# Neighbourhood attention in pairs of heads: the exponential's bias from the pass with the maximum, one split and one transposition for two heads

## The chip, the cores and the metric

The kernel runs on one core of one Trainium2 chip. The metric is the device time of one execution in microseconds (us); lower is better. TensorE (PE) multiplies matrices, VectorE (DVE), ScalarE (ACT) and GpSimd (POOL) work on elements, and SyncE (SP) issues DMAs. PE reads from SBUF and writes to PSUM.

## The reference

One encoder layer over 1024 tokens of width 1024, a grid of 16 rows and 64 columns. The normalised input is projected to two head groups: group A is grouped-query attention, group B is neighbourhood attention with 8 heads of 64. Each group is gated, the two are concatenated and projected, the residual is added and a final norm follows. Group B, cut to what matters:

```python
k_rows = lax.dynamic_slice_in_dim(kg, r0, kh, axis=1)      # 8 rows of keys for a query row
sc = jnp.einsum('bjqhd,bkjchd->bhjqkc', qb, k_band) * scale
sc = jnp.where(mask, sc + bias, -jnp.inf)                  # learned bias by 2-D offset, 16 columns
p = jax.nn.softmax(sc, axis=(-2, -1))
o = jnp.einsum('bhjqkc,bkjchd->bjqhd', p, v_band)
o_b = o_b * jax.nn.silu(g_b)
mixed = jnp.concatenate([o_a, o_b], axis=-1)
x = x + mixed @ w_out
```

## The kernel before

Numbers are kept as pairs of 16-bit floats, a high part and a low part, and a product takes three matmuls: high by high, high by low, low by high. Tokens are cut into 8 units of 128 queries (`u`). In group B a unit sees its own 128 keys and those of the two units beside it: 384 keys, or 256 for the first and the last unit. The order is `ORDER`, units 0, 7, 1, 2, 3, 4, 5, 6, and the 8 heads of a unit one after the other. The first sixteen heads are so the narrow ones.

The stage of group B is 64 steps, one for a head, with a tail of 6. A step is written by `Flow.step` and `run_units`:

- `b_qk` makes the scores of two heads at once on PE (in every other step; `sb` tiles, four PSUM banks). For its own head DVE adds the bias of the offsets, keeps the sum `t` and takes its maximum (L825), and multiplies the maximum by minus the scale and adds a constant (L827, 128x1). ACT takes the exponential twice from `t`: as 32-bit `p32` (L828) and as 16-bit high part (L829).
- `b_lo` of the head before subtracts the two on DVE for the low part (L834). SP then issues one DMA that transposes both parts (L838, 6 blocks of 128x128) into a `ptb` place.
- Jobs that are due on DVE, then filling matmuls on PE (L482, in chunks of six; `FILL_B_END` chunks a step, the rest carried over): gate projections (`pj` tiles) and then output projections (`po` tiles), which share two PSUM buffers.
- `b_pv`, five heads later (six from step `MORE` on), multiplies the transposed parts with the values on PE (L851 to L853). After the fourth head of a group DVE divides by the sum and POOL multiplies with the gate.

Within a stage each engine does its instructions in the order in which the steps write them. Work that is not attention stands in lists of jobs: `job(engine, cost, ..., delay)` puts it into the step that lies `delay` steps ahead, jobs of ACT at the start of that step and jobs of DVE after `b_lo`; `BASE_B` says how much of a step is left for those that may wait. Three kinds of job matter here:

- A filling tile that is done is emptied one step later: for a gate ACT takes tanh (L682) and DVE multiplies (L687); for an output DVE adds to the residual (L961). The tile after the next one takes its buffer.
- `os_start` prepares a finished unit for the output projection. Squares (ACT L888, DVE L892) and a power on POOL, then ACT writes the two halves of the high part (L900), one step apart, and DVE the low halves behind them (L904). Then two DMAs transpose the parts of `mhl` (L913), and the output tiles of that unit can begin. `SPLIT_AT` says in which step it starts.
- Weights of a later group are squared (ACT L350), and split into high (ACT L392) and low parts (DVE L397), a quarter at a time.

Of the kernel before, what the change touches and what calls it, by code (L numbers as in the profile page):

```python
# [16 lines left out]
P = 128  # L17
KC = 8
NU = 8
# [15 lines left out]
PREP = {2: 4, 3: 0, 4: 2}  # L35
NEG = -1.0e38
EPS = 1e-6
# [101 lines left out]
def kernel(ctx: ExitStack, tc: tile.TileContext, x: bass.AP, w: bass.AP, wo: bass.AP,  # L139
# [203 lines left out]
    def squares(g, delay):  # L343

        wss[g] = [tn(f"wss{g}_{k}", 1, "ws") for k in range(4)]

        def quarter(i):
            o = (carve(ar, 16384 + SLOTS["th"][0] + (0 if "six" in late else (turn.get("th", 0) + 1) % 2) * SLOTS["th"][1], [512], BF16)
                 if "b" in late else va_more)
# [329 lines left out]
    def g_gen(g, up, mix, cols, isb):  # L679
        def evac(pt):  # L680
            th = slot("th" if "b" in late else "tha", [P, 2, GC], F32)
            job("act", 0.7, lambda: act.activation(th, pt, AF.Tanh, scale=col(G2 + g - GATE)), late=0)  # L682
# [129 lines left out]

    def b_qk(i, u, h):
        hh, h4i = divmod(h, 4)
# [6 lines left out]
        hl = t.bitcast(F16).rearrange("p (a b) -> p a b", a=2)  # L821
        assert ("bias", int(0 < u < NU - 1), hh, h4i) in ready
        b = bias[hh][:, h4i, (a - u + 1) * P:(a - u + 1 + n) * P]
        mx = tn(f"mx{u}_{h}")
        dve.tensor_tensor_reduce(out=t, in0=s, in1=b, scale=1.0, scalar=-3e38,  # L825
                                 op0=OP.add, op1=OP.max, accum_out=mx)
        dve.tensor_scalar(mx, mx, col(NSB + hh), LN_P, op0=OP.mult, op1=OP.add)  # L827
        act.activation(p32, t, AF.Exp, bias=mx, scale=col(SCB + hh))  # L828
        act.activation(hl[:, 0], t, AF.Exp, bias=mx, scale=col(SCB + hh))  # L829
        hls["b", u, h] = (hl, p32)  # L830

    def b_lo(i, u, h):
        hl, t = hls.pop(("b", u, h))
        dve.tensor_tensor(hl[:, 1], t, hl[:, 0], op=OP.subtract)  # L834
        k = i - MORE + 5
        pt = (area(32896, [2 * keys(u)[1], P], F16) if k >= 0 and k % 6 == 5 else
              slot("ptb", [P, 2 * keys(u)[1], P], F16))
        sp.dma_start_transpose(pt, hl.rearrange("p a b -> p (a b)"))  # L838
        pts["b", u, h] = pt

    def b_pv(i, u, h):
        hh = h // 4
# [5 lines left out]
        o = pv["b", u, hh][:, h % 4]  # L848
        pt = pts.pop(("b", u, h))
        for c in range(n):  # L850
            pe.matmul(o, pt[:, c], vb[hh][:, a + c, h % 4, v_hi], start=c == 0, stop=False)  # L851
            pe.matmul(o[:, :D], pt[:, c], vb[hh][:, a + c, h % 4, v_lo], start=False, stop=False)
            pe.matmul(o, pt[:, n + c], vb[hh][:, a + c, h % 4, v_hi], start=False, stop=c == n - 1)  # L853
        if h % 4 == 3:
            def evac():
# [5 lines left out]
                dve.tensor_tensor(s4, s4, col(VF + 4 * hh, 4), op=OP.mult)  # L861
                ot = slot("ob", [P, 4, D], F32)
                dve.tensor_tensor(ot, pv["b", u, hh][:, :, :D], s4[:, :, None].to_broadcast([P, 4, D]), op=OP.mult)
# [224 lines left out]

    def run_units(units, skew, qk, lo, pvf, n, hooks=None, by_hand=0, more=1000):

        m, hand = len(units), ExitStack()
        for i in range(m + skew + (more < 1000)):
            back = skew + (i >= more)
            if i == by_hand:
                hand.enter_context(tc.manual_schedule(engines={e.engine for e in (act, dve, pool, sp)}))
            first = (lambda: qk(i, *units[i])) if i < m else None
            second = (lambda: lo(i - 1, *units[i - 1])) if 1 <= i <= m else None
            last = (lambda: pvf(i - back, *units[i - back])) if i >= back and i != more else None
            if qk is a_qk:
                first, last = (lambda f=first, l=last: [g() for g in (f, l) if g]), None  # L1100
            if hooks:
                hooks(i)
            fl.step(n(i), first, second, last)
            sums_now()
        return hand
# [9 lines left out]
    fl.base = BASE_A  # L1115
    with run_units(ua, SKEW_A, a_qk, a_lo, a_pv, rates(FILL_A + [(64 - n_head, mid)], FILL_A_END), by_hand=HAND):
        pass
# [11 lines left out]

    ub = [(u, h) for u in ORDER for h in range(NH)]  # L1130

    late["b"] = True
    def hooks(i):
        if i == 0:
            late["r"] = [one.tile([P, 3072], F16, tag=f"r{j}", name=f"rest{j}") for j in range(2)]
            outer, late["inner"] = [t[:, 2048:2816].bitcast(F32) for t in late["r"]]
            make = load_bias(1, outer)
            sp.dma_start(late["inner"], headmask)
            for h in range(4):
                job("dve", 0.5, make, h, delay=h, late=0)  # L1140
        if i == 1:
            prep(13)
        if NH < i <= 2 * NH:
            at(1, "post", narrow, i - NH - 1)
        if i == 46:
            late["gout"] = one.tile([P, 1024], F32, tag="gain", name="gain_o")
            sp.dma_start(late["gout"], dap(gain_out, 0, [[0, P], [1, 1024]]))
# [17 lines left out]
    def hooks2(i):  # L1165
        hooks(i)
        if i == MORE - 2:
            late["six"] = True
        for u, k in zip(ORDER, SPLIT_AT):
# [5 lines left out]
    fl.base = BASE_B  # L1175
    with run_units(ub, SKEW_B, b_qk, b_lo, b_pv, rates(FILL_B, FILL_B_END), hooks2, more=MORE):
        pass
# [92 lines left out]
```

## Time and profile before

| | us |
|---|---|
| median of 3 runs (572.87 to 575.61) | 575.24 |
| span of the profiled execution, first to last instruction | 570.8 |
| own time of the profiled execution | not printed; 2 to 5 above its span if it was like the three runs |
| stage of group B, first maximum to last product with the values | 370.8 to 536.4 |
| PE busy over the span | 517.2 (91%) |
| DVE busy | 459.4 (80%) |
| ACT busy | 391.7 (69%) |
| mean granted clock of PE | 0.979 |

Busy times are sums of records. A PE that is recorded as busy is not always at its peak, and an instruction of DVE may start some hundredths of a microsecond before the one ahead of it ends. A wait is put down to the engine that ended last before it. The chain that ended last is mostly a list of small pieces here, so the stage is best read from waits, from the source views and from the timeline.

### The profile page before, as it was taken

What the parts mean: (1) busy time and instruction counts of PE and PEld (TensorE: products, weight loads), DVE (VectorE), ACT (ScalarE), POOL (GpSimd) and SP (SyncE); (2) the same over time, 40 slices, a digit from 0 to 9 for tenths busy, and PEclk for the clock granted to TensorE, in tenths of its full rate; (3) what the DMA queues carried; (4) which work ended last, traced back from release to release, by engine and by line L of the source; (5) the groups of instructions that cost most, each with busy time, mean ns of one, the idle gap of its engine ahead of it and who ended that gap; (6) DMA issues with size and microseconds to landing.
All of it is one profiled execution on the core that took longest, in us unless ns stands there. A gap on an engine that the chain in (4) does not pass through costs nothing. (4 is left out here: it accounts for less than half of the span.)

```text
span 570.8 us, 13962 instructions
## 1 busy us (share of the span) xinstructions
PE 517.2 (91%) x5583; PEld 402.1 (70%) x5583; DVE 459.4 (80%) x1018; ACT 391.7 (69%) x615; POOL 150.6 (26%) x181
## 2 busy tenths in 40 slices
PE   2678889969999999999999999999799799997994
PEld 0456777757887555568888888887677577776883
DVE  4688787989887988778779887589978998988852
ACT  5546457667777769687696886387888888875321
POOL 2395786650000000000000022334521311212210
PEclk9979999998999999999999999999989899999998
DMA  8999548779999989998998999436466999899842
GB/s 241 220 175 231 121 91 185 131 144 165 220 180 210 158 204 200 197 196 162 217 191 192 184 160 213 132 52 130 121 121 107 198 216 165 144 176 167 194 109 73
DMA packets 245539, 95.49 MB, mean 167 GB/s; under 512 B 236513, under 2 KB 237025, under 8 KB 243554
## 3 DMA queue, kind: packets, MB, share of 16 engines
q1 hardware_dynamic: 241874, 73.89, 71.1%
q0 software_dynamic: 3312, 19.92, 12.7%
q10 hardware_dynamic: 288, 0.79, 0.5%
q8 instruction: 43, 0.70, 0.5%
q14 instruction: 22, 0.18, 0.1%
HBM read 29.56 MB, written 4.19 MB: 59 GB/s over the span
## 5 line engine op out<-in xcount | busy, mean ns | idle before, releaser
L482 PE MATMUL pj<-whl,hT 128*128 128x256 f16 x2112 | 254.9, 278 | 26.1 <-DMA hT<-ar 9.2
L482 PEld LDWEIGHTS <-hT 128*128 128x128 f16 x2112 | 203.7, 99 | 63.6 <-issue 20.3
L722 ACT ACTIVATE ar<-s,nm,sm 128x1024 f32<-128x1024 f32 x64 | 76.9, 1201 | 56.5 <-DVE nm L720 56.2
L720 DVE CUSTOM_DVE_ANT_0 ar<-s,sm 128x1024 bf16<-128x1024 f32 x64 | 82.0, 1281 | 35.0 <-PE s L715 34.6
L482 PEld LDWEIGHTS <-ar 128*128 128x128 f16 x768 | 73.0, 99 | 16.1 <-issue 7.0
L728 DVE TENSOR_TENSOR ar<-ar 128x1024 f16<-128x1024 f32 x64 | 80.3, 1255 | 0.9 <-ACT ar L723 0.8
L482 PE MATMUL po<-whl,ar 128*128 128x256 f16 x576 | 68.7, 273 | 2.0 <-DVE x2b L961 1.8
L723 ACT ACTIVATE ar<-ar 128x1024 f16<-128x1024 f32 x64 | 67.6, 1057 | 1.9
L828 ACT ACTIVATE rq<-ar,mx,sm 128x384 f32<-128x384 f32 (+1 forms) x64 | 43.0, 672 | 25.3 <-DVE mx L827 25.0
L829 ACT ACTIVATE ar<-ar,mx,sm 128x384 f16<-128x384 f32 (+1 forms) x64 | 43.5, 680 | 2.1
L482 PE MATMUL kb<-hT,whl 128*128 128x512 f16 x192 | 44.5, 379 | 0.0
L834 DVE TENSOR_TENSOR ar<-rq,ar 128x384 f16<-128x384 f32 (+1 forms) x64 | 35.5, 555 | 8.2 <-ACT ar L829 8.0
L746 PE MATMUL pv<-va,ar 128*128 128x64 f16 x384 | 40.6, 195 | 0.0
L745 PE MATMUL pv<-va,ar 128*128 128x65 f16 x384 | 40.5, 194 | 0.0
L747 PE MATMUL pv<-va,ar 128*128 128x65 f16 x384 | 40.4, 193 | 0.0
L713 PE MATMUL s<-kTa,rq 128*128 128x512 f16 x128 | 38.5, 383 | 1.5 <-ACT ar L722 1.4
L745 PEld LDWEIGHTS <-ar 128*128 128x128 f16 x384 | 35.9, 97 | 5.5 <-issue 0.3
L397 DVE SCALAR_TENSOR_TENSOR whl<-raw,sm,whl 128x512 f16<-128x512 f32 x52 | 39.5, 790 | 0.0
L746 PEld LDWEIGHTS <-ar 128*128 128x128 f16 x384 | 35.7, 98 | 5.5 <-issue 0.3
L207 POOL DMA_DIRECT2D raw<-in_w_dram x11 | 6.7, 607 | 113.0 <-ACT ar L723 88.8
L747 PEld LDWEIGHTS <-ar 128*128 128x128 f16 x384 | 35.7, 99 | 0.0
L392 ACT ACTIVATE whl<-raw,sm 128x512 f16<-128x512 f32 x52 | 33.9, 708 | 0.0
(163 smaller groups left out, 918.8 us busy)
## 6 DMA issues: line engine op xcount, KB each, us to landing
raw<-in_w_dram POOLq DMA_DIRECT2D x11, 1024.0 KB, 7.4
raw<-in_wo_dram POOLq DMA_DIRECT2D x4, 1024.0 KB, 5.7
ar<-in_x_dram SPq DMA_DIRECT2D x7, 512.0 KB, 6.3
khh<-ar SPq DMA_DIRECT2D x16, 128.0 KB, 3.5
x2b<-in_x_dram POOLq DMA_DIRECT2D x4, 512.0 KB, 6.1
x<-in_x_dram POOLq DMA_DIRECT2D x4, 512.0 KB, 5.8
out_dram<-x2b SPq DMA_DIRECT2D x8, 256.0 KB, 4.8
ar<-ar SPq DMA_TRANSPOSE x112, 4.3
```

The source lines that it names most:

```text
L397: dve.scalar_tensor_tensor(wp[g][1][:, q], raw[g][:, q], col(S_ + g), wp[g][0][:, q], op0=OP.mult, op1=OP.subtract)
L482: pe.matmul(*o[0], **o[1])
L713: pe.matmul(s[:, c * 512:(c + 1) * 512], q, kTa[:, 4 * c:4 * c + 4, hh], start=True, stop=False)
L720: dve.tensor_tensor_reduce(out=hl[:, 1].bitcast(BF16), in0=s, in1=col(SHA).to_broadcast([P, 1024]), scale=col(NSA), scalar=3e38, op0=OP.ad ...
L722: act.activation(p32, s, AF.Exp, bias=nm, scale=col(SCA))
L723: at(0, "mid", lambda: act.activation(hl[:, 0], p32, AF.Copy))
L728: dve.tensor_tensor(hl[:, 1], p32, hl[:, 0], op=OP.subtract)
L745: pe.matmul(o, pt[:, kt], va[:, kt, hh, v_hi], start=kt == 0, stop=False)
L746: pe.matmul(o[:, :D], pt[:, kt], va[:, kt, hh, v_lo], start=False, stop=False)
L747: pe.matmul(o, pt[:, 8 + kt], va[:, kt, hh, v_hi], start=False, stop=kt == 7)
L828: act.activation(p32, t, AF.Exp, bias=mx, scale=col(SCB + hh))
L829: act.activation(hl[:, 0], t, AF.Exp, bias=mx, scale=col(SCB + hh))
```

## The change

Group B goes by pairs of heads: 32 steps with a tail of 3. For each head DVE's pass now multiplies the sum by minus the scale and takes the minimum, which is the bias of the exponential as it stands, so the multiplication on 128x1 is gone. ACT takes one exponential per head, into a 32-bit `p32` for both heads, and then one scaled 16-bit copy of both. DVE makes one low part for the pair. One DMA transposes four parts (12 blocks, or 8 in narrow units). In a step the low part of the pair before stands ahead of the maxima, and no longer behind. The values follow two pairs later (three from `MORE` on). Places in SBUF are laid out anew: three for `t` and for `ptb`, each for a pair, one for `p32`, one for `th`, and `qkg` takes the scratch of the squares and of the division.

```diff
-BASE_A, BASE_B = (1.8, 2.6, 2.9), (0.8, 0.9, 1.0)
+BASE_A, BASE_B = (1.8, 2.6, 2.9), (1.6, 1.4, 1.7)
-SKEW_A, SKEW_B = 5, 5
+SKEW_A, SKEW_B = 5, 2
-FILL_B_END = 2.4
-MORE = 40
-SPLIT_AT = (8, 16, 24, 32, 40, 48, 56)
+FILL_B_END = 4.8
+MORE = 20
+SPLIT_AT = (4, 8, 12, 16, 20, 24, 28)
-         "t": (0, 1536, 5), "ptb": (7680, 1536, 5), "ob": (15360, 1024, 1), "th": (16384, 16512, 2), "tha": (32896, 2048, 1), "y": (16384, 2048, 1),
-         "p32": (AREA + 14464, 1536, 2)}
+         "t": (0, 3072, 3), "ptb": (9216, 3072, 3), "th": (32896, 2048, 1), "y": (32896, 2048, 1),
+         "p32": (AREA + 14464, 3072, 1)}
...
-        if h % 2 == 0:
-            b_scores(u, (h, h + 1))
-        s = sbs.pop((u, h))
-        t, p32 = slot("t", [P, w], F32), slot("p32", [P, w], F32)
...
-        dve.tensor_tensor_reduce(out=t, in0=s, in1=b, scale=1.0, scalar=-3e38,
-                                 op0=OP.add, op1=OP.max, accum_out=mx)
-        dve.tensor_scalar(mx, mx, col(NSB + hh), LN_P, op0=OP.mult, op1=OP.add)
-        act.activation(p32, t, AF.Exp, bias=mx, scale=col(SCB + hh))
-        act.activation(hl[:, 0], t, AF.Exp, bias=mx, scale=col(SCB + hh))
+        b_scores(u, (2 * p, 2 * p + 1))
+        t, p32 = slot("t", [P, 2, w], F32), slot("p32", [P, 2, w], F32)
+        for e in range(2):
...
+            dve.tensor_tensor_reduce(out=t[:, e], in0=sbs.pop((u, h)), in1=b, scale=col(NSB + hh), scalar=3e38,
+                                     op0=OP.add, op1=OP.min, accum_out=nm)
+            act.activation(p32[:, e], t[:, e], AF.Exp, bias=nm, scale=-1.0)
+        p32 = p32.rearrange("p e k -> p (e k)")
+        act.activation(hl[:, 0], p32, AF.Copy, scale=2.0 ** 14)
...
-        dve.tensor_tensor(hl[:, 1], t, hl[:, 0], op=OP.subtract)
...
-        sp.dma_start_transpose(pt, hl.rearrange("p a b -> p (a b)"))
+        dve.scalar_tensor_tensor(hl[:, 1], p32, 2.0 ** 14, hl[:, 0], op0=OP.mult, op1=OP.subtract)
+        pt = slot("ptb", [P, 4 * keys(u)[1], P], F16)
+        sp.dma_start_transpose(pt, hl.rearrange("p a k -> p (a k)"))
...
+    def parts_b(i, back):
+        def first():
+            if 1 <= i <= 32:
+                b_lo(*ub[i - 1])
+            if i < 32:
+                b_qk(*ub[i])
+        return first, None, (lambda: b_pv(*ub[i - back])) if i >= back and i != MORE else None
```

Group A's steps are written through a function `parts_a` in the same order as before.

On DVE in unit 3, before: head 5 (`mx3_5`) with its maximum, the multiplication, the low part of head 4, and behind it the addition that empties the output tile `po0_13`.

```order
L825 ISA ar_78,mx3_5_6448<-sb0_5107,rq_79 128x384
L825 ISA mx3_5_6448 128x1
L827 TENSOR_SCALAR mx3_5_6448<-mx3_5_6448,sm_97 128x1
L834 TENSOR_TENSOR ar_78<-rq_79,ar_78 128x384
L961 SCALAR_TENSOR_TENSOR x2b_6284<-po0_13_6307,rw0_13_6308,x2b_6284 128x256 x2
```

The same engine after: the low part of the pair of heads 4 and 5, the maxima of heads 6 and 7 (`nm3_6`, `nm3_7`), then that addition.

```order
L833 SCALAR_TENSOR_TENSOR ar_78<-rq_79,ar_78 128x768
L824 ISA ar_78,nm3_6_6402<-sb1_5108,rq_79,sm_97 128x384
L824 ISA nm3_6_6402 128x1
L824 ISA ar_78,nm3_7_6405<-sb1_5108,rq_79,sm_97 128x384
L824 ISA nm3_7_6405 128x1
L963 SCALAR_TENSOR_TENSOR x2b_6243<-po0_13_6210,rw0_13_6211,x2b_6243 128x256 x2
```

The addition moved from behind head 5 to behind heads 6 and 7; on PE the tile `po1_13`, which takes the same buffer, begins in the step of heads 6 and 7 in both kernels. The second place is the low part of the mixed row of unit 2 (`mhl2`) on DVE, before, in head 1 of unit 4:

```order
L825 ISA ar_78,mx4_1_6602<-sb0_5107,ar_78 128x384
L825 ISA mx4_1_6602 128x1
L827 TENSOR_SCALAR mx4_1_6602<-mx4_1_6602,sm_97 128x1
L834 TENSOR_TENSOR ar_78<-rq_79,ar_78 128x384
L904 SCALAR_TENSOR_TENSOR mhl2_6501<-ar_78,os2_6500,mhl2_6501 128x512
```

And after, in the pair of heads 4 and 5 of unit 4:

```order
L367 TENSOR_SCALAR wss16_0_6165<-sb0_5107 128x1
L824 ISA ar_78,nm4_4_6602<-sb0_5107,rq_79,sm_97 128x384
L824 ISA nm4_4_6602 128x1
L824 ISA ar_78,nm4_5_6605<-sb0_5107,rq_79,sm_97 128x384
L824 ISA nm4_5_6605 128x1
L963 SCALAR_TENSOR_TENSOR x2b_6243<-po1_13_6438,rw1_13_6439,x2b_6243 128x256 x2
L906 SCALAR_TENSOR_TENSOR mhl2_6412<-ar_78,os2_6411,mhl2_6412 128x512
```

The last low half of `mhl2` moved from head 1 to behind heads 4 and 5, while PE begins the first output tile of unit 2, `po2_13`, with heads 6 and 7 of unit 4 in both kernels, after six matmuls of the tile ahead of it.

More of the change, by code (lines that the diff above doesn't have):

```diff
@@ L1087, with run_units @@
         mixA[up] = carve(ar, MIX + 4096 * up, [2, 512], F32)
-    def run_units(units, skew, qk, lo, pvf, n, hooks=None, by_hand=0, more=1000):
-        m, hand = len(units), ExitStack()
+    def run_units(m, skew, parts, n, hooks=None, by_hand=0, more=1000):
+        hand = ExitStack()
         for i in range(m + skew + (more < 1000)):
-            back = skew + (i >= more)
             if i == by_hand:
                 hand.enter_context(tc.manual_schedule(engines={e.engine for e in (act, dve, pool, sp)}))
[L1096 to L1100, printed above, removed]
             if hooks:
                 hooks(i)
-            fl.step(n(i), first, second, last)
+            fl.step(n(i), *parts(i, skew + (i >= more)))
             sums_now()
@@ L1115, with parts_a @@
     fl.base = BASE_A
-    with run_units(ua, SKEW_A, a_qk, a_lo, a_pv, rates(FILL_A + [(64 - n_head, mid)], FILL_A_END), by_hand=HAND):
+    def parts_a(i, back):
+        def first():
+            if i < 64:
+                a_qk(i, *ua[i])
+            if i >= back:
+                a_pv(i - back, *ua[i - back])
+        return first, (lambda: a_lo(i - 1, *ua[i - 1])) if 1 <= i <= 64 else None
+    with run_units(64, SKEW_A, parts_a, rates(FILL_A + [(64 - n_head, mid)], FILL_A_END), by_hand=HAND):
         pass
@@ L1139, in hooks @@
             for h in range(4):
-                job("dve", 0.5, make, h, delay=h, late=0)
+                job("dve", 0.5, make, h, delay=h // 2, late=0)
         if i == 1:
             prep(13)
-        if NH < i <= 2 * NH:
-            at(1, "post", narrow, i - NH - 1)
-        if i == 46:
+        if 4 < i <= 8:
+            for e in range(2):
+                at(1, "post", narrow, 2 * (i - 5) + e)
+        if i == 23:
             late["gout"] = one.tile([P, 1024], F32, tag="gain", name="gain_o")
```

54 lines of the change are left out of this document (27 added, 27 removed).

## The prediction, made before the changed kernel was run

> **What bounds the kernel now.** I read the page first: TensorE (PE) is busy for nine tenths of the span, so only idle or slowed PE time can be won.
>
> ```profile
> span 570.8 us, 13962 instructions
> PE 517.2 (91%) x5583; PEld 402.1 (70%) x5583; DVE 459.4 (80%) x1018; ACT 391.7 (69%) x615; POOL 150.6 (26%) x181
> ```
>
> The change touches the stage of group B alone, from about 370 us. The view by stretches shows the engines in its wide part.
>
> ```profile
> 402.00:527.00 125.00, 114.18 (x1255) 89.69 (x1252) 111.20 (x350) 100.78 (x180) 28.81 (x39) 0.97 0.87 160
> ```
>
> Columns after the times: PE, weight loads, VectorE (DVE), ScalarE (ACT), POOL, granted clock. DVE is busy 111 of 125 us, PE 114: two engines are near full. The view of waits for 366 to 540 us says who waits:
>
> ```profile
> ACT rq L828 <- DVE mx L827: 25.0, 23, 2.9
> DVE ar L834 <- ACT ar L829: 8.0, 15, 1.2
> ```
>
> ```profile
> PE pvb L851 <- DMA ar<-ar: 5.5, 4, 2.3
> PE pj L482 <- DVE ar L687: 3.2, 2, 2.9
> ```
>
> PE waits for transposes that follow a late low part of DVE, and for DVE to empty a projection tile. So DVE is what PE waits for, and DVE's own chain runs through ACT. I take the stage by pairs of heads, numbered 0 to 31 as they run; a pair starts with its scores on PE (timeline, weight loads):
>
> ```profile
> 402.36 0.23 PEld L804 LDWEIGHTS <-qTb 128*128 128x128 f16 x2
> 470.51 0.13 PEld L804 LDWEIGHTS <-qTb 128*128 128x128 f16 x2
> 475.04 0.13 PEld L804 LDWEIGHTS <-qTb 128*128 128x128 f16 x2
> 516.59 0.13 PEld L804 LDWEIGHTS <-qTb 128*128 128x128 f16 x2
> ```
>
> ```profile
> 441.29 1.47 PE L482 MATMUL pj<-whl,hT 128*128 128x256 f16 x12
> 443.98 2.14 PE L482 MATMUL pj<-whl,hT 128*128 128x256 f16 x18
> ```
>
> These are the starts of pairs 8, 21, 22 and 31. Pair 21 ran unhindered in 4.53 us with 30 filling matmuls; six cost 2.14 - 1.47 = 0.67. Of pairs 8 to 30, five have 24 (2.4 chunks per head, rounded). Unhindered they need 18 x 4.53 + 5 x 3.86 = 100.8 us; they took 516.59 - 402.36 = 114.2. So 13.4 us are lost there, and two waits after them add 1.5 + 1.6:
>
> ```profile
> 521.26 0.49 PE L482 MATMUL po<-whl,ar 128*128 128x256 f16 x3 [1.54 <-DVE x2b L961]
> 528.18 0.20 PE L851 MATMUL pvb<-rq,ar 128*128 128x65 f16 x1 [1.62 <-DMA ar<-ar]
> ```
>
> Together 16.5 us, the most that this stage can return. Part of it is clock: after the wait that ends at 450.56 the granted clock (second column from the DMA's two) fell.
>
> ```profile
> 450.55 0.10 PEld L851 LDWEIGHTS <-ar 128*128 128x128 f16 x1 [2.62 <-DMA ar<-ar]
> 450.00:452.00 2.00, 1.44 (x15) 0.74 (x16) 1.89 (x5) 1.97 (x5) 0.00 (x0) 0.82 1.18 106
> 452.00:454.00 2.00, 2.00 (x11) 1.41 (x10) 1.35 (x6) 1.97 (x5) 0.00 (x0) 0.50 0.93 217
> 454.00:456.00 2.00, 2.00 (x24) 1.69 (x22) 1.97 (x8) 1.74 (x3) 1.88 (x3) 0.82 1.11 201
> ```
>
> 2 x (0.18 + 0.50 + 0.18) = 1.7 us of PE for one wait of 2.6 us.
>
> **The change, part by part.** Prices from the view of groups:
>
> ```profile
> L825 DVE CUSTOM_DVE_ANT_0 ar<-sb,rq 128x384 f32<-128x384 f32 x24 | 13.2, 550 | 1.4 <-DMA ar<-ar 1.4
> L825 DVE CUSTOM_DVE_ANT_0 ar<-sb,ar 128x256 f32<-128x256 f32 x8 | 3.3, 414 | 0.0
> L825 DVE DVE_READ_ACCUMULATOR2_ANT mx<- 128x1 f32 x64 | 5.2, 82 | 0.0
> L827 DVE TENSOR_SCALAR mx<-mx,sm 128x1 f32<-128x1 f32 x64 | 13.7, 214 | 2.3
> L834 DVE TENSOR_TENSOR ar<-rq,ar 128x384 f16<-128x384 f32 x48 | 27.2, 567 | 4.9 <-ACT ar L829 4.9
> L720 DVE CUSTOM_DVE_ANT_0 ar<-s,sm 128x1024 bf16<-128x1024 f32 x64 | 82.0, 1281 | 35.0 <-PE s L715 34.6
> L687 DVE SCALAR_TENSOR_TENSOR ar<-ar,pj 128x512 f32<-128x512 f32 x8 | 5.5, 684 | 1.4 <-ACT ar L682 1.2
> L397 DVE SCALAR_TENSOR_TENSOR whl<-raw,sm,whl 128x512 f16<-128x512 f32 x52 | 39.5, 790 | 0.0
> L828 ACT ACTIVATE rq<-ar,mx,sm 128x384 f32<-128x384 f32 x48 | 33.5, 699 | 18.6 <-DVE mx L827 18.4
> L829 ACT ACTIVATE ar<-ar,mx,sm 128x384 f16<-128x384 f32 x48 | 33.9, 707 | 1.6
> L723 ACT ACTIVATE ar<-ar 128x1024 f16<-128x1024 f32 x64 | 67.6, 1057 | 1.9
> L562 ACT ACTIVATE ar<-ar 128x512 f16<-128x512 f32 x8 | 5.0, 631 | 7.0 <-POOL ar L547 7.0
> L961 DVE SCALAR_TENSOR_TENSOR x2b<-po,rw,x2b 128x256 f32<-128x256 f32 x16 | 7.0, 476 | 0.0
> ```
>
> DVE, per wide pair. The small multiplication L827 goes: -2 x 0.214. The pass with the maximum now takes its scale from a column: L825 grows by (550 - 414)/128 = 1.06 ns an element, so with a constant 1024 would take 1.23 us; L720, which has a column, takes 1.28, so +0.06 each. Two low parts of 0.567 become one over 768 elements: between 684 x 1.5 = 1.03 (L687) and 790 x 1.5 = 1.19 (L397, some of them beside POOL) if nothing in it is fixed, and 0.684 + 256 x 1.06 ns = 0.96 if the slope alone counts; I take 0.97. Before: 2 x (0.55 + 0.08 + 0.21 + 0.57) = 2.82; after: 2 x (0.61 + 0.08) + 0.97 = 2.35. That is -0.47 a pair, some 15 us over 32.
>
> ACT: a second exponential per head (0.707) becomes one copy of both: between L562 and L723, 0.84. Before 2.81, after 2 x 0.70 + 0.84 = 2.24, or 2.1 if the constant scale shortens the exponential: -0.57, 18 us over 32 pairs. SP issues 32 transposes of 12 blocks for 64 of 6:
>
> ```profile
> L838 SPq DMA_TRANSPOSE ar<-ar x64: 1188/1215/4018, 374.1 to 529.6; - x64
> DMA to landing us min/median/max: 2.4/3.2/7.6
> ```
>
> ```profile
> L733 SPq DMA_TRANSPOSE ar<-ar x48: 1461/1918/5082, 94.9 to 353.7; - x48
> DMA to landing us min/median/max: 4.2/4.6/8.8
> ```
>
> ```profile
> L865 POOL TENSOR_TENSOR ar<-ar 128x256 f32<-128x256 f32 x16 | 15.1, 943 | 70.8 <-DVE ar L863 56.2 <-DVE rw L970 8.5 <-DVE of L988 6.0
> ```
>
> With 16 blocks landing takes 4.6, with 6 it takes 3.2; for 12 I take 4.1. The product with the values comes two pairs later, a slack of nearly 4 us, so I cost this at nothing; a landing over 8 us would show. The scratch `qkg`, now shared by ACT's squares, DVE's division and POOL's product behind it, can make one of them wait for another; such a wait is at most the 0.94 us of one product on POOL (the row of L865), twice a unit, and the old scratch had one place as well: nothing. The transposes of `mhl` queue on SP behind a pair's transposition of some 1.6 us instead of 1.2, at most 0.4 later.
>
> None of this is PE's own work: matmuls and their order by pair are the same. What PE gets depends on two prices that the trace does not show.
>
> First, the coupling. DVE now runs low part, two maxima, other jobs; the low part waits for the copy, the copy for both exponentials. The closed chain, 0.97 + 0.69 + 2 x 0.70 + 0.84 = 3.9 us, stays under PE's 4.53: free in a quiet pair. In a crowded one the pair costs DVE 2.35 plus its jobs, or ACT 2.2 plus its jobs, and the gain in a quiet pair is only 0.6 us. Crowded, by the order: pair 14 (a gate product, a set of sums, three low parts of weights, about 4.4 us of jobs; ACT has 3.6 before it), 17 (about 4.6), 23 and 28 (4.0, 3.8), 29 to 31 (3.0 to 3.6).
>
> Second, the delays are counted in steps, and a step is now a pair. An output tile is added in the step after its last matmul, and the low half of a mixed row comes three steps after its start. Let lag be how much later than 1.0 us after the scores DVE begins its first maximum. Carried from pair to pair by the durations above, it is about 1.5 us at pair 14, 4.1 at 18, 3.5 at 19, 0.8 at 22, 2.0 at 29, 2.8 at 31. The places where PE then waits:
> - Pair 14: `pj12_2` takes the buffer of `pj11_2` after 24 matmuls, 3.3 us into the pair; DVE multiplies that tile at 1.0 + 1.15 + 0.68 plus lag 1.5 = 4.3: 1.0 late.
> - Pair 19: `po1_13` starts after 24 matmuls, at 0.7 + 24 x 0.11 = 3.3. DVE empties `po0_13` after two maxima and the addition, 1.0 + 1.2 + 0.9 = 3.1 plus lag 3.5: 3.3 late. The low half of `mhl1` ends in pair 18 at 1.0 + 1.2 + 1.6 + 4.1 = 7.9 and lands 4.1 later, 7.5 into pair 19: 4.2 late. The later of both counts, 4.2.
> - Pair 23: `po2_13` starts after six matmuls, at 1.35. The low half of `mhl2` ends in pair 22 at 1.0 + 1.2 + 2.0 + 0.8 = 5.0, lands at 9.1, 4.6 into pair 23: 3.2 late. Before, it stood four heads earlier and PE did not wait there.
> - Pair 29: addition of `po1_15`, 3.1 + 2.0 - 3.3 = 1.7.
> - After pair 31: by the same sum about 1.6.
>
> That is 11.7 us. The waits at 19 and 23 are longer than the 2.6 above, so each costs 1.7 of clock; the slower PE lets DVE catch up, so I let the last two waits, 3.3 together, halve: net 3.4 - 1.7 = 1.7. Sum: -16.5 + 11.7 + 1.7 = -3.1 us.
>
> Bounds: no new wait but the 2.4 that pair 23 has at no lag gives -14; if the low part takes its upper 1.19 us and jobs run beside POOL at the length seen in
>
> ```profile
> 409.64 1.22 DVE L834 TENSOR_TENSOR ar<-rq,ar 128x256 f16<-128x256 f32 x1
> 410.77 1.48 DVE L904 SCALAR_TENSOR_TENSOR mhl<-ar,os,mhl 128x512 f16<-128x512 f32 x1
> ```
>
> the crowded pairs each lose 1 to 1.5 us more, and the sum is +4.
>
> The Trainium skill, "TensorE: Matmul & The Clock Gate", in its section "Why this matters for your kernels", says that idle gaps of PE should stay under about 3 us or the clock goes back to half. By it the wait at 23 hardly costs clock, and the sum would be 1.7 lower, -4.8; the 2.6 us wait quoted above shows half clock after a shorter gap, and I go by that row.
>
> Tail: after the last product with the values the same 234 matmuls follow, and DVE and ACT have room there; I cost it at nothing. The page prints no own time of the profiled execution; its span of 570.8 lies 4.4 under the median 575.24, about what lies around a span if that run was a median one. From 575.24 the sum gives 572.1.
>
> **Rivals.**
> - *Full gain.* With 15 us off DVE the lag stays near zero and only pair 23 waits: -14, 561. For it: ACT's 25.0 us of waiting for L827 shows the removed operation on the chain. Against it: pairs 14 and 17 exceed 4.53 on both engines.
> - *The waits only move.* If lag is 0.8 us larger at four places, 11.7 becomes 15: -0.5 to +1, 575. For it: the new deadlines forgive less than the old, and in pair 8 of the present kernel, scores at 402.36, DVE's first maximum starts 6.5 us behind them:
>
> ```profile
> 408.90 0.56 DVE L825 CUSTOM_DVE_ANT_0 ar<-sb,ar 128x384 f32<-128x384 f32 x1
> ```
>
> - *Slower.* One mechanism: the doubled step makes PE wait for mixed rows and full tiles at 14, 19, 23, 29 and the end. It decides from 16.5 us in sum, 3.3 each at five places. With 22 us it gives 580. Against it: a PE that waits lets DVE catch up.
> - *No cheaper copy:* the copy's two sizes bracket it between 0.63 and 1.06 us; nothing speaks for it.
>
> **How the numbers follow.** A measurement here tells about 0.5% (2.9 us) from no change. My case (569 to 572.4): 0.36. Full gain: 0.12, so faster 0.48. Moved waits: 0.30. Slower: 0.22. The range runs from 563 to 579, leaving out about one in ten on each side; the forecast's own range is 569 to 574.
>
> **What would show it.** No row for the small multiplication; 32 low parts near 0.97 us; ACT's copy near 0.84; DVE's busy share in the stage down by a tenth; pairs without jobs at 4.53 us. PE waits for `mhl` transposes and `x2b` additions near the starts of `po1_13` and `po2_13`, with half clock behind them. I am wrong if those starts do not wait (then faster), or if PE waits in quiet pairs for the transposes of the weights of attention themselves (then the chain of 3.9 us is longer than I think).

## The result and the profile after

The changed kernel took 589.69 us (median of 4 runs, 589.44 to 590.79), the kernel before, on the same chip, 574.12. The recorded ratio is 1.0296, with a 95% interval of 1.0266 to 1.0327; the two medians alone give 1.0271. It is slower by some 3%, where I had forecast 572.1 in a range of 563 to 579.

The page of the kernel after, its first lines:

```profile
span 588.1 us, 13785 instructions
PE 525.1 (89%) x5583; PEld 406.7 (69%) x5583; DVE 449.3 (76%) x922; ACT 368.2 (63%) x583; POOL 156.0 (27%) x181
```

DVE has 10.1 us less work than before and ACT 23.5 less, and yet the span is 17.3 longer. The groups of the kernel after, shapes apart, are close to the prices of the prediction or under them:

```profile
L826 ACT ACTIVATE rq<-ar,nm 128x384 f32<-128x384 f32 x48 | 26.8, 605 | 38.4 <-DVE nm L824 38.4
L833 DVE SCALAR_TENSOR_TENSOR ar<-rq,ar 128x768 f16<-128x768 f32 x24 | 24.9, 1039 | 10.5 <-ACT ar L828 10.5
L828 ACT ACTIVATE ar<-rq 128x768 f16<-128x768 f32 x24 | 20.2, 843 | 0.8
L824 DVE CUSTOM_DVE_ANT_0 ar<-sb,rq,sm 128x384 f32<-128x384 f32 x24 | 13.8, 611 | 3.2 <-PE sb L806 3.2
```

Columns: busy time of the group, mean ns of one, idle time of the engine just ahead and what ended it. So the work is not the cause; the idle columns are. The stage from the scores of pair 8 to those of pair 31, first of the kernel before (402.36 to 516.59), then of the kernel after (405.70 to 538.69), in the view by stretches:

```profile
402.36:516.59 114.23, 105.40 (x1160) 82.46 (x1157) 102.02 (x321) 94.66 (x169) 27.00 (x35) 0.97 0.84 157
```

```profile
405.70:538.69 132.99, 110.81 (x1155) 85.12 (x1152) 95.34 (x252) 80.42 (x151) 32.13 (x36) 0.91 0.82 140
```

The same pairs take 18.8 us more. PE's idle time grows by 13.4 (8.8 to 22.2), and its busy time by 5.4 for the same matmuls, with the mean granted clock at 0.91 instead of 0.97. Another 3.2 us is lost before pair 8, and what follows the start of pair 31 is 4.8 shorter. Where PE waited, from its timeline after (start, duration, instruction, idle time and what ended it):

```profile
399.59 0.20 PE L853 MATMUL pvb<-rq,ar 128*128 128x65 f16 x1 [2.32 <-DMA ar<-ar]
438.83 0.83 PE L481 MATMUL pj<-whl,hT 128*128 128x256 f16 x6 [1.93 <-DVE ar L686]
456.21 0.24 PE L853 MATMUL pvb<-ar 128*128 128x65 f16 x1 [3.63 <-DMA ar<-ar]
469.70 1.04 PE L481 MATMUL po<-rest,ar 128*128 128x256 f16 x6 [2.18 <-DVE x2b L963]
491.37 0.61 PE L481 MATMUL po<-rest,ar 128*128 128x256 f16 x2 [6.26 <-DMA ar<-mhl]
507.98 0.20 PE L853 MATMUL pvb<-ar 128*128 128x65 f16 x1 [3.06 <-DMA ar<-ar]
530.96 1.44 PE L481 MATMUL po<-rest,ar 128*128 128x256 f16 x6 [3.71 <-DVE x2b L963]
```

These stand in pairs 6, 14, 17, 19, 23, 25 and 29. Four are the ones that the prediction named (14, 19, 23, 29). The three at `pvb`, where the product with the values waits for a transposition of a pair (L835), 9.0 us together, it had costed at nothing; the kernel before had 5.5 us of such waits, and the prediction let them go. The three transpositions were issued at 392.9, 447.2 and 492.9 us and landed after 6.7, 9.0 and 15.0 us, and each had a load of weights or of x beside it. The view of waits (366 to 560 us) shows the engines behind that:

```profile
ACT rq L826 <- DVE nm L824: 48.8, 19, 7.7
...
DVE ar L833 <- ACT ar L828: 14.3, 14, 2.4
...
DVE ar L824 <- DMA ar<-ar: 6.6, 1, 6.6
...
DVE x2b L963 <- DMA x2b<-in_x_dram: 5.8, 2, 3.0
...
PE pvb L853 <- DMA ar<-ar: 9.0, 3, 3.6
...
PE po L481 <- DMA ar<-mhl: 6.5, 2, 6.3
PE po L481 <- DVE x2b L963: 5.9, 2, 3.7
```

ACT waits 48.8 us for a maximum where it waited 25.0, DVE 14.3 for the copy where it waited 8.0 for the second exponential, and DVE once 6.6 us (pair 25) because the place of the scores was still being transposed, by the same DMA of 15.0 us.

### The profile page after: what moved, and what is told of

Its sections match the earlier page's. It is cut to its first block, busy times and chain, and to the rows that moved or that the text cites. A ratio compares the mean times of both kernels' runs of the same rounds, so it can differ in the third digit from the quotient of the medians.

```text
span 588.1 us, 13785 instructions
## 1 busy us (share of the span) xinstructions
PE 525.1 (89%) x5583; PEld 406.7 (69%) x5583; DVE 449.3 (76%) x922; ACT 368.2 (63%) x583; POOL 156.0 (27%) x181
## 4 chain that ended last, share of the span: by engine, by line
PE 55%; DMA 13%; DVE 11%; issue 7%; POOL 6%; ACT 5%; SPq 1%; POOLq 0%; DVEq 0%; ACTq 0%
PE pj L481 24%; PE kb L481 7%; PE po L481 6%; DMA ar<-ar 6%; PE s L712 4%; PE s L714 4%; PE pv L745 3%; PE pv L744 2%; PE pv L746 2%; DMA ar<-in_x_dram 2%; DMA ar<-mhl 2%; POOL nt L534 2%; DMA raw<-in_w_dram 2%; DVE ar L824 1%; DVE ar L301 1%
## 5 line engine op out<-in xcount | busy, mean ns | idle before, releaser
L481 PEld LDWEIGHTS <-hT 128*128 128x128 f16 x2112 | 205.8, 100 | 63.9 <-issue 17.5
L481 PEld LDWEIGHTS <-ar 128*128 128x128 f16 x768 | 76.8, 102 | 28.0 <-DMA ar<-mhl 8.7
L826 ACT ACTIVATE rq<-ar,nm 128x384 f32<-128x384 f32 (+1 forms) x64 | 34.0, 578 | 49.5 <-DVE nm L824 48.8
L833 DVE SCALAR_TENSOR_TENSOR ar<-rq,ar 128x768 f16<-128x768 f32 (+1 forms) x32 | 31.0, 970 | 14.3 <-ACT ar L828 14.3
L867 POOL TENSOR_TENSOR ar<-ar,qkg 128x256 f32<-128x256 f32 x16 | 17.2, 1076 | 89.1 <-DVE qkg L865 89.1
L744 PEld LDWEIGHTS <-ar 128*128 128x128 f16 x384 | 35.9, 97 | 5.5 <-issue 0.3
L745 PEld LDWEIGHTS <-ar 128*128 128x128 f16 x384 | 35.7, 98 | 5.5 <-issue 0.3
L481 PE MATMUL po<-rest,ar 128*128 128x256 f16 x192 | 27.5, 304 | 12.5 <-DMA ar<-mhl 6.5
L746 PEld LDWEIGHTS <-ar 128*128 128x128 f16 x384 | 35.8, 99 | 0.0
```

The costliest lines, as they stand in the source:

```text
L481: pe.matmul(*o[0], **o[1])
L744: pe.matmul(o, pt[:, kt], va[:, kt, hh, v_hi], start=kt == 0, stop=False)
L745: pe.matmul(o[:, :D], pt[:, kt], va[:, kt, hh, v_lo], start=False, stop=False)
L746: pe.matmul(o, pt[:, 8 + kt], va[:, kt, hh, v_hi], start=False, stop=kt == 7)
L826: act.activation(p32[:, e], t[:, e], AF.Exp, bias=nm, scale=-1.0)
L833: dve.scalar_tensor_tensor(hl[:, 1], p32, 2.0 ** 14, hl[:, 0], op0=OP.mult, op1=OP.subtract)
```

## The experiments

Theories: the delays counted in steps have doubled (T1); the low part ahead of the maxima puts DVE and ACT in lock-step (T2); one transposition for a pair is issued later and lands later (T3). The table gives each run's ratio to runs of the kernel before on the same chip (the rows come from several chips), and the time from the first scores of the stage (pair 0) to those of pair 31 in the profiled execution. The ratio says how fast a kernel is; the stage says where, free of what happens ahead of it.

| kernel | median us | ratio, 95% interval | stage us |
|---|---|---|---|
| before | 574.12 | 1 | 146.8 |
| new arithmetic, by heads (`e1_by_heads`) | 562.14 | 0.9847 (0.9809 to 0.9884) | 140.4 |
| the same in the new places (`e12c`) | 559.08 | 0.9766 (0.9734 to 0.9798) | 139.4 |
| and two heads' transpositions joined (`e12`) | 567.76 | 0.9925 (0.9895 to 0.9955) | 144.1 |
| and low part and copy joined, low part behind the maxima from pair 11 (`e21`) | 574.72 | 1.0009 (0.9979 to 1.0039) | 149.7 |
| and low part ahead of the maxima throughout (`e15`) | 578.53 | 1.0117 (1.0066 to 1.0168) | 155.9 |
| and the product two pairs behind (`e3`) | 582.48 | 1.0183 (1.0131 to 1.0235) | 159.0 |
| and steps of a pair: the changed kernel | 589.69 | 1.0296 (1.0266 to 1.0327) | 168.7 |

Read downwards it is the change put on piece by piece. The first piece gains; each piece of the pairing loses. For `e1_by_heads` 569 to 575 us had been expected if the arithmetic is worth what its rows say, and 576 to 582 if it costs lock-step by heads; it took 562.14, better than both. The intervals of neighbours are apart except those of `e15` and `e3`, so that piece alone (+0.7%) is not settled. The stages go the same way: -6.4, -1.0, +4.7, +5.6, +6.2, +3.1, +9.7, together +21.9.

**Steps of a head, the work of a pair.** The pair's work stands in every second step, and all delays and `SPLIT_AT` are those of the kernel before; the budgets of `BASE_B` are half those of the changed kernel (0.8, 0.7, 0.85 where the kernel before has 0.8, 0.9, 1.0).

```diff
+        p, e = divmod(i, 2)          # low part and maxima in even steps only
...
+        q = p - 2 - (i >= MORE)      # product of head e of pair q
...
-    with run_units(32, SKEW_B, parts_b, rates(FILL_B, FILL_B_END), hooks2, more=MORE):
+    with run_units(64, SKEW_B, parts_b, rates(FILL_B, FILL_B_END), hooks2, more=MORE):
```

> The changed kernel with the work of a pair unchanged (same instructions, same places in memory, one transposition of a pair), but the delays counted in steps of one head again: a pair is two steps, with half the filling and one head's values in each. Delays in steps (T1): the loads of x, the chain of a mixed row and the emptying of tiles come as early as in the kernel before, so the PE waits at pairs 14, 19, 23 and 29 (2.2, 2.5, 6.5 and 4.0 us) shrink to under 1.5 us each; 572 to 579 us. Lock-step (T2) or late transpositions (T3): those waits keep half or more of their length, 585 to 590 us, and the waits for a transposition at pairs 17 and 25 (3.9 and 3.3 us) stay whatever the rest does.

It took 582.48 us: the ratio went from 1.0296 to 1.0183, the stage from 168.7 to 159.0. That lies between T1's figure and the others'. Its waits (366 to 560 us) show that both have a part:

```profile
PE pvb L853 <- DMA ar<-ar: 19.1, 8, 4.6
PE po L481 <- DMA ar<-mhl: 1.6, 2, 0.8
```

The waits for mixed rows and for `x2b` (6.5 and 5.9 us after) shrink to 1.6 and none, as T1 said. But a PE that comes earlier now meets the transpositions of pairs, eight times instead of three, 19.1 us.

**The product three pairs behind.** The kernel above with

```diff
-MORE = 40
+MORE = 0
...
-        q = p - 2 - (i >= MORE)
+        q = p - 3
```

> The kernel with steps of a head and the work of a pair (582.5 us) with the product of values three pairs behind its scores from the start, not only from pair 20 on. Its waits for a transposition ahead of pair 20 were 2.7, 2.6, 2.0, 3.2, 1.5 and 4.9 us. If they are there because two pairs leave a transposition, issued 8 to 10 us after the scores and 4 us under way, too little: they go, 568 to 575 us. If transpositions are late for another reason (DVE's lag, the queue): they move one pair on and stay, 579 to 585 us.

573.75 us, ratio 1.0002 (0.9971 to 1.0032), stage 149.1. The waits for a pair's transposition fall from 19.1 to 3.3, and what is late next is the mixed row, which also starts one step later here up to step 40 (`MORE` = 0):

```profile
PE po L481 <- DMA ar<-mhl: 7.6, 2, 5.8
PE pvb L853 <- DMA ar<-ar: 3.3, 3, 1.9
```

**Five heads behind.** The kernel of steps of a head again, with the product where it stands by heads:

```diff
-        q = p - 2 - (i >= MORE)
+        q, e2 = divmod(i - back, 2)  # back is 5, and 6 from step MORE on
```

> The kernel with steps of a head and the work of a pair (582.5 us), with the product of each head's values five heads behind its scores as in the kernel by heads (six from head 40 on) instead of two pairs: half a pair later for both heads of a pair, half a pair earlier than the kernel of three pairs (573.8 us). If the place of the product is what stands between 582.5 and the kernel by heads with a joined transposition (567.8 us): 567 to 573 us. If it is the joined low part, its copy and the order on DVE (lock-step, T2): 576 to 582 us.

578.53 us: nearer to the second figure than to the first. Half a pair of slack is worth 3.1 us in the stage; the interval overlaps with that of the kernel it was made from, and 16.7 us of waits for transpositions are left. So putting the product where it stands by heads does not return the bulk of the 14.7 us that were open (582.48 against 567.76).

**The transposition in two.** The changed kernel with the high parts transposed by a DMA of their own.

```diff
+        sp.dma_start_transpose(pt[:, :2 * n], hl[:, 0])     # behind the copy, in `b_qk`
...
-        sp.dma_start_transpose(pt, hl.rearrange("p a k -> p (a k)"))
+        sp.dma_start_transpose(pt[:, 2 * n:], hl[:, 1])     # behind the low part
```

> The changed kernel with the transposition of a pair split in two: the high parts are transposed right behind the scaled copy, the low parts behind the low part's subtraction (64 transpositions of 6 blocks instead of 32 of 12). Late transpositions (T3): the waits at pairs 6, 17 and 25 (2.6, 3.9, 3.3 us of PE, and 6.6 us of DVE for the place of a transposition) fall to under 1 us each; 577 to 582 us. Delays in steps (T1) or lock-step (T2): within 2 us of the changed kernel, 588 to 592 us.

614.13 us, which says nothing of T3: from pair 20 on the high parts went into a place whose former values the product had still to use, so that it waited for the transposition of a later pair and used that pair's values: this kernel does not compute the layer. The next kernel issues them at the end of the step from pair 20 on.

> The changed kernel with the transposition of a pair split in two of 6 blocks: the high parts behind the scaled copy (from pair 20 on at the end of the step, when their place has been read), the low parts behind the low part's subtraction. Late transpositions (T3), if it is the size of one transposition that lands late: the waits for one at pairs 6, 17 and 25 (2.6, 3.9, 3.3 us) halve, 580 to 586 us. If it is when the low part is ready and how far behind the scores the product of values stands: no gain, since the second half is issued when the whole was, 588 to 593 us.

584.45 us, ratio 1.0196 (1.0152 to 1.0241): 1% off the changed kernel, inside T3's figure. The waits at `pvb` fall from 9.0 to 4.7 us. That it is the size of a transposition is not shown by this: up to pair 19 the split also issues the high parts earlier. Put on the kernel of three pairs, the same split (the high parts at the end of the pair's second step):

> The kernel with steps of a head and the product of values three pairs behind (573.8 us), with the transposition in two of 6 blocks: the high parts at the end of the pair's second step, the low parts behind the low part. Late transpositions (T3): 565 to 571 us, the waits of 6.1 us at 458 and 2.2 us at 524 halved. If the loss that is left is elsewhere: 572 to 577 us.

568.92 us, ratio 0.9912 (0.9886 to 0.9938), again about 1%. Its profiled execution took 575.59 us and shows no such gain (stage 149.7, waits at `pvb` 5.7 us for 3.3), so where the gain lies is not shown.

**The joined transposition alone.** By heads first, in the changed kernel's places (`e12c`), then with this edit alone (`e12`):

```diff
         if h % 2 == 0:
...
+            return
...
-        sp.dma_start_transpose(pt, hl.rearrange("p a b -> p (a b)"))          # every head, 6 blocks
...
+        sp.dma_start_transpose(pt, pr.bitcast(F16).rearrange("p e k -> p (e k)"))   # two heads, 12 blocks
```

> The kernel by heads with the new arithmetic (562.1 us), every operation, step and transposition as there, but in the changed kernel's places: three places of a pair for scores and transposed values instead of five of a head, one for the tanh of a gate instead of two, the scratch of the table qkg for what is multiplied into a gated row. A control for the next kernel. If the places cost nothing: 560 to 566 us. If the one place of the tanh or the three places of a pair hold work up: 568 to 576 us.

> The kernel of the control, by heads in all its operations and steps, with one thing of the pairing alone: the transpositions of two heads are one of 12 blocks, issued behind the low part of the second head. Late transpositions (T3): the first head's values come one head, about 2.2 us, later, and the whole lands about 1 us later than one of 6 blocks; the product of values waits for it 10 us or more in the stage, 568 to 576 us. If what is left of the loss is the pair's low part or the order on DVE, not the transposition: within 2 us of the control.

559.08 and 567.76 us. The places cost nothing (one place for `th`, three of a pair, `qkg` as scratch: if anything a gain), and the joined transposition, with the later issue of its first head, costs 1.6%. The waits of PE for it, without and with:

```profile
PE pvb L854 <- DMA ar<-ar: 5.0, 4, 2.6
```

```profile
PE pvb L856 <- DMA ar<-ar: 10.9, 6, 4.5
```

The landings say how little slack there is. The source view of the transpositions of wide units, in the kernel before and then after, for 408 to 437, 436 to 466 and 466 to 540 us (time from issue to landing):

```profile
DMA to landing us min/median/max: 2.7/2.8/5.6
...
DMA to landing us min/median/max: 2.7/5.8/7.6
...
DMA to landing us min/median/max: 2.7/4.4/7.6
```

```profile
DMA to landing us min/median/max: 3.6/3.7/4.3
...
DMA to landing us min/median/max: 3.7/6.3/12.2
...
DMA to landing us min/median/max: 3.6/6.0/15.0
```

In the first window no load is in flight but one of weights, up to 413 us in the kernel before; there 12 blocks land in 3.7 us and 6 in 2.8, where the prediction had 4.1 and 3.2 (its 3.2 is a median over the whole stage, units of 4 blocks and times of loads included). In the other two, with loads of weights and of x in flight much of the time, the median is 6.3 and 6.0 us after and 5.8 and 4.4 before; the longest doubles from 7.6 to 15.0. A load does this to a narrow pair too: the transposition of 8 blocks that PE waited for in pair 6 took 6.7 us beside a load of weights from 391.6 to 398.6 us, where the three recorded before it took 3.0.

**The order on DVE.** By heads, the kernel of 559.08 us with the low part ahead of the maximum:

```diff
-        return ((lambda: b_qk(*ub[i])) if i < 64 else None, (lambda: b_lo(*ub[i - 1])) if 1 <= i <= 64 else None,
+        return ((lambda: b_lo(*ub[i - 1])) if 1 <= i <= 64 else None, (lambda: b_qk(*ub[i])) if i < 64 else None,
```

> The control by heads (559.1 us) with one thing changed: the low part of the head before stands ahead of this head's maximum on DVE, as in the changed kernel, instead of behind it. Lock-step (T2): the low part waits for ACT's copy, the maximum behind it comes later and with it ACT's exponential, so the two engines take turns; DVE's wait for the copy grows from 5 to 15 us or more and the time to 564 to 575 us. If the order costs nothing: within 2 us of the control.

582.34 us, ratio 1.0166 (1.0122 to 1.0210): this one exchange costs 4% and is slower than any theory had it. The waits of the control and then of this kernel:

```profile
ACT rq L826 <- DVE nm L824: 28.3, 26, 3.5
DVE ar L833 <- ACT ar L827: 5.2, 12, 0.9
```

```profile
ACT rq L826 <- DVE nm L824: 50.3, 44, 3.4
DVE ar L833 <- ACT ar L827: 29.0, 43, 1.3
```

Two steps of it, DVE and then ACT:

```profile
427.83 0.60 DVE L824 CUSTOM_DVE_ANT_0 ar<-sb,rq,sm 128x384 f32<-128x384 f32 x1
429.68 0.56 DVE L833 SCALAR_TENSOR_TENSOR ar<-rq,ar 128x384 f16<-128x384 f32 x1 [1.24 <-ACT ar L827]
430.16 0.61 DVE L824 CUSTOM_DVE_ANT_0 ar<-sb,rq,sm 128x384 f32<-128x384 f32 x1
```

```profile
428.48 0.62 ACT L826 ACTIVATE rq<-ar,nm 128x384 f32<-128x384 f32 x1 [1.43 <-DVE nm L824]
429.13 0.52 ACT L827 ACTIVATE ar<-rq 128x384 f16<-128x384 f32 x1
```

Maximum, exponential, copy, low part, next maximum: a ring in which each engine stands still while the other works. It turns in 430.16 - 427.83 = 2.33 us with no job in it, and PE needs 4.53 / 2 = 2.27 per head. A job put between two of these instructions lengthens it.

In pairs the order was turned back from pair 11 on, with a second place for the exponentials, in three settings: the changed kernel, the kernel of three pairs, and that of five heads.

```diff
+        two = k > 10 and k % 2       # k is the number of the pair
+        p32 = rr[:, :, 2048:2816].bitcast(F32)[:, :, :w] if two else slot("p32", [P, 2, w], F32)
...
-            if 1 <= p <= 32:
+            if 1 <= p <= 10:
                 b_lo(*ub[p - 1])
...
                 b_qk(*ub[p])
+            if 10 < p <= 32:
+                b_lo(*ub[p - 1])
```

These are the lines of the last two; the first has the same in steps of a pair.

> The changed kernel with a second place for the exponentials of a pair, and from pair 11 on the low part of the pair before stands behind the two maxima instead of ahead of them. Lock-step (T2): DVE's wait of the low part for ACT's copy (14.3 us in the stage) falls under 6 us, the maxima come about 1 us earlier, and the time falls to 575 to 583 us. Delays in steps (T1): the waits for x2b and for the mixed rows stay, 587 to 592 us. Late transpositions (T3): the transposition is issued later still by about 1.2 us, so 590 to 596 us.

> Steps of a head, product of values three pairs behind, and from pair 11 on the low part behind the two maxima with a second place for the exponentials: the three remedies together, the arithmetic and the transposition of a pair kept. If the loss of pairing was these three: at or under the kernel by heads with the new arithmetic, 556 to 564 us. If pairing costs on its own (one late transposition holds two heads): 566 to 575 us.

> Steps of a head, the work of a pair, the product of values five heads behind (578.5 us), and from pair 11 on the low part behind the two maxima, with a second place for the exponentials. It differs from the kernel by heads with a joined transposition (567.8 us) by the joined low part and copy alone from there on. If the order costs pairs what it costs heads (23 us over 64 steps of lock-step, T2): 566 to 573 us. If pairs lose little by the order, because a pair's low part waits for one copy and not for two (5.4 us of DVE's waiting in the stage): within 3 us of 578.5, or slower, since the transposition is issued about 1.2 us later.

582.96 us (1.0198, 1.0174 to 1.0222), 581.97 (1.0121, 1.0056 to 1.0185) and 574.72 (1.0009, 0.9979 to 1.0039). In the first and the third the order, with the second place that it needs, is worth 1%; in the changed kernel DVE's wait for the copy falls from 14.3 to 6.0. The second, slower than either figure expected for it, had mixed rows as what was late already. There it costs 1%: PE's waits for `mhl` grow from 7.6 to

```profile
PE po L481 <- DMA ar<-mhl: 14.2, 4, 6.2
```

So T2 holds, but what it is worth in pairs depends on what comes late next, and the three remedies do not add up.

**Loads of x earlier.** The changed kernel with one step instead of two ahead of each load of x:

```diff
-        at(2, "end", turn_x2, u)
+        at(1, "end", turn_x2, u)
...
-            at(2, "end", next_load)
+            at(1, "end", next_load)
```

> The changed kernel with the delays of the x loads alone halved: two steps become one, from the mixed row's transposition to the load and from one load to the next, as long in time as in the kernel before. Delays in steps (T1): the load that held DVE 3.0 us at pair 23 is issued about 4.5 us earlier, so the 6.5 us of PE there and the 4.0 us at pair 29 shrink by 3 to 8 us together, 580 to 586 us. If the rows themselves (their chain of steps, and DVE behind the low parts) hold the tiles: 587 to 591 us.

602.37 us, ratio 1.0468 (1.0397 to 1.0539): the opposite. The wait of DVE for a load (5.8 us) was no reason to load earlier. In the trace that wait is gone, but the four loads into `x2b` are issued within 10.3 us (452.7 to 463.0), loads of x land after up to 20.3 us, and PE's waits for transpositions of pairs grow from 9.0 to 16.0 us and those for mixed rows from 6.5 to 12.2. That the crowd of loads holds the transpositions up is argued from this and from the landings above; it was not tried by itself.

**More and less slack by heads.** The control of 559.08 us with the product six heads behind from head 24 on, and with five throughout:

```diff
-MORE = 40
+MORE = 24        # and in the other kernel MORE = 1000
```

> The kernel of the control (by heads, new arithmetic, places of pairs) with the product of values six heads behind its scores from head 24 on instead of from 40 on, for which the three places of a pair have room. In the kernel by heads PE waited 3.8 us for a transposition at 440 us, while loads were in flight. If the slack of a transposition sets what is left: 556 to 561 us. If the loads hold the mixed rows there anyway: within 2 us of the control.

> The control by heads with the product of values five heads behind throughout; there it falls to six from head 40 on. One step less, and mixed rows one head earlier from head 40 on: about -2 us if transpositions still land in time (555 to 558 us), 560 to 565 us if the later ones, which share the DMA engines with the loads of x, are then late.

564.58 us (0.9854, 0.9815 to 0.9893) and 563.94 (0.9852, 0.9811 to 0.9893): both slower than the control, and that with six slower than either figure expected. With six the wait for transpositions falls from 5.0 to 1.6 us, but mixed rows come later and PE waits 5.1 for them. With five the former is 5.7, and 2.3 us of a new wait for an addition come to it; that is not all of the 4.9 us lost. The control stands between. It is the best version found, 2.3% faster than the kernel before.

## Why the prediction was wrong

*The prices: right.* The maximum's pass is 0.611 us (0.61 predicted), the joined low part 1.04 (0.97), the copy 0.843 (0.84), L827 is gone; the exponential is 0.605 where I took 0.70. What I did not work out is how much of this needs the pairing. By heads the low part takes 0.593 and the copy 0.523 each, from these groups of `e1_by_heads`:

```profile
L833 DVE SCALAR_TENSOR_TENSOR ar<-rq,ar 128x384 f16<-128x384 f32 x48 | 28.5, 593 | 2.9 <-ACT ar L828 2.8
L828 ACT ACTIVATE ar<-rq 128x384 f16<-128x384 f32 x48 | 25.1, 523 | 1.5
```

Joining them saves 2 x 0.593 - 1.039 = 0.15 us of DVE a pair and 2 x 0.523 - 0.843 = 0.20 of ACT. The rest of the gain comes by heads, and the arithmetic alone brought 1.5%.

*"The product with the values comes two pairs later, a slack of nearly 4 us, so I cost this at nothing": the step that failed.* I compared one landing time, 4.1 us, with one slack. The transposition is issued behind the low part of the pair: in the first two waits PE was ready for it 4.4 and 5.4 us after its issue, and it landed after 6.7 and 9.0; in the third, three pairs behind, 12.0 and 15.0. Over the assumed 4.1 us the first two left 0.3 and 1.3 us, and not nearly 4. Landings over 8 us, the prediction's own sign, came from the transposition of pair 15 on. The term cost 9.0 us of waits as the kernel stands and 19.1 once other waits were gone; by itself the joining costs 1.6%.

*"Free in a quiet pair": failed in size.* The closed chain of 3.9 us is under 4.53, as said, but jobs lie inside it, not beside it. The order cost 4% by heads and 1% in pairs.

*The doubled delays: right in place, in half of the places for another reason.* The waits at pairs 14, 19, 23 and 29 were forecast as 1.0, 4.2, 3.2 and 1.7 (1.8 by its own terms), and were 1.9, 2.2, 6.3 and 3.7: 14.1 against 10.1. After pair 31, where 1.6 was forecast, PE did not wait. At 14 and 29 DVE was behind, as said: its lag was 2.6 and 4.2 us, where I had 1.5 and 2.0. At 19 it was not. The wait at pair 17 had let it catch up; its first maximum began 0.8 us behind the scores, where I had 4.5, and then it stood at an addition for a load of x:

```profile
464.83 0.62 DVE L824 CUSTOM_DVE_ANT_0 ar<-sb,rq,sm 128x384 f32<-128x384 f32 x1 [2.30 <-PE sb L806]
469.16 0.48 DVE L963 SCALAR_TENSOR_TENSOR x2b<-po,rw,x2b 128x256 f32<-128x256 f32 x1 [2.77 <-DMA x2b<-in_x_dram]
```

The mixed row `mhl1`, the later of the two in the prediction, was not late by DVE either: its low half was done 3.9 us into pair 18, where I had 7.9. But its two transpositions landed 9.6 and 6.4 us after their issue, at 469.4 and 470.0 us, so that PE would have waited almost as long for them. At 23 DVE stood 3.0 us for a load too, ahead of the low half of `mhl2`; but what ended PE's 6.26 us was the high half, transposed from 484.8 us on in 6.5 us, where I had 4.1 for a landing. The low half, which the third matmul needs, held PE 0.26 us more:

```profile
492.24 1.01 PE L481 MATMUL po<-rest,ar 128*128 128x256 f16 x4 [0.26 <-DMA ar<-mhl]
```

So the right place was in part luck: at 19 and 23 late DMAs made the wait, and not a DVE behind its time. Loads of x stand two steps behind a mixed row, so the doubled step delays them as well, which I had not counted. Undoing the steps returned 1.1 of the 3.0%. The rival "slower" named the doubled step, with 580 us; the two other mechanisms it did not have.

*The clock: 3.4 forecast, for two waits; about 10 measured.* In the control by heads, at a granted clock of 1.00, PE is busy for 101.3 us from pair 8 to pair 31; in the kernel before it was 105.4 (0.97), after 110.8 (0.91).

```profile
398.63:506.55 107.92, 101.28 (x1160) 81.13 (x1157) 95.98 (x274) 82.43 (x169) 28.87 (x37) 1.00 0.94 170
```

In the kernel after, five of the seven waits are followed by a stretch at 0.50 to 0.58, where I had two. After the wait of 2.32 us at 399.59 PE ran four microseconds at little over half clock; after the one of 2.18 at 469.70 it lost nothing, nor did the control after one of 2.64 at 442.57 (last line):

```profile
400.00:402.00 2.00, 2.00 (x16) 1.20 (x13) 2.00 (x4) 0.00 (x0) 1.26 (x1) 0.56 0.00 0
402.00:404.00 2.00, 2.00 (x13) 1.48 (x12) 1.88 (x6) 1.00 (x3) 1.87 (x3) 0.58 0.47 57
470.00:472.00 2.00, 1.94 (x29) 1.34 (x29) 0.73 (x2) 1.86 (x5) 0.00 (x0) 1.00 0.55 123
```

```profile
444.00:446.00 2.00, 2.00 (x27) 1.83 (x25) 1.86 (x6) 1.97 (x5) 0.55 (x1) 1.00 0.92 229
```

The rule of about 3 us in the Trainium skill ("TensorE: Matmul & The Clock Gate", "Why this matters for your kernels") is too kind by the first of these; waits of 2.2 to 2.6 us went either way here. (The 2.6 us of the prediction are the idle time of the weight loads; PE itself had stood 2.34 us there.)

*The sum.* Against the prediction's unhindered 100.8 us, pairs 8 to 30 took 133.0: 6.7 of waits at `pvb` (forecast 0), 14.1 at the four places (forecast 10.1, or 9.3 with the last of them halved), 1.4 of other idle time, and 10.0 of longer busy time (forecast 3.4 of clock). Of the miss of 19.5 us the waits put at nothing are 6.7, the clock 6.6 and the four places 4.8; all three waits at `pvb` have the low clock behind them, of the four others those at 23 and 29.

*Still open:* the 0.8% between `e12` and `e21` holds the joined low part and copy, the work of two heads in one step, the other budgets of `BASE_B`, and lock-step in the first ten pairs, which were not told apart; and nothing separates how much of a late transposition is its size and how much its neighbours on the DMA engines.

## What to carry to other kernels

Before work of two units is joined, count what the joining alone saves (here 0.15 us of DVE a pair), and set against it that every delay counted in steps, every place and every transfer now has twice the grain. Do not put the consumer of another engine's result ahead of the producer of that engine's next input: the exchange of two instructions in one engine's order cost 23 us by heads. A slack is to be compared with the transfer's longest landing while loads run, not with its median.

## What the runs showed of the hardware

The exponential of 128x384 took 0.605 us with a constant scale and 0.699 with its scale in a column of SBUF (L826 after, L828 before); the maximum's pass went the other way, 0.611 with a column and 0.550 with a constant. A transposition of 12 blocks is not twice one of 6 (3.7 against 2.8 us to landing with next to no load in flight), but its longest, with loads in flight, is (15.0 against 7.6).
